# Up-weight sums kept in DRAM for the second token half, and the FFN's stores moved to the load queue

## The chip, the cores and the metric

The kernel runs on one core of one Trainium2 chip. The metric is the device time of one execution in microseconds (us); for the kernel before it is the median of three runs. TensorE (PE) does the matrix products, VectorE (DVE), ScalarE (ACT) and GpSimd (POOL) the elementwise work, and SyncE (SP) issues DMAs.

## The reference, cut to what matters

One layer of a diffusion backbone over 2048 tokens of width 1024. The first part (modulated RMSNorm, an input projection, neighbourhood attention, a gating block, a convolution block, an output projection, a residual) is not touched by the change. The second part is the FFN:

```
h2 = modulate(rmsnorm(x, norm2_g), mod_l[3], mod_l[4])        # 2048 x 1024
gate, up = split(h2 @ w_up, 2, axis=-1)                       # w_up: 1024 x 5632
gate = dwconv(gate, conv_w, conv_b)                           # 3 taps along the tokens
x = x + mod_l[5] * ((silu(gate) * up) @ w_down)               # w_down: 2816 x 1024
return rmsnorm(x, final_norm_g)
```

All arrays are float32. The kernel splits each float32 operand into a high part (a rounded copy) and a low part (what is left), and a product is made of three matmuls: high by high, high by low, low by high.

## The kernel before, in words

The FFN works on the tokens in two halves, `t` = 0 and 1, of 1024 tokens, which are two blocks of 512. The 44 column tiles of `w_up` (22 of the gate, 22 of up) are taken two by two: tile `c0` and tile `c0 + 11`. With the two blocks of tokens and the two halves of the 1024 input features this makes a 2 by 2 by 2 block product, and it is computed with seven products in place of eight (Winograd's form of Strassen's scheme). `winograd` issues the seven, each as twelve matmuls of 128 by 128 by 512 (`up_prod`, L1310), in the order B11, T2, T1, T3, B21, T4, B22. One such block of a gate tile and one of an up tile make a pair (`up_pair`), and there are eleven pairs in each half: 22 x 2 x 7 x 12 = 3,696 matmuls.

The scheme needs sums of the weights. `up_weights` loads the two tiles (`wa`, `wb`, 512 KB each, a double buffer), and POOL makes four sums `s1` to `s4` of 128 x 512 from their quarters (L1295 to L1298), through a ring `ws` of three buffers. Then each of the seven weight operands (three quarters as they are, four sums) is split by `halves`: ACT writes the high part (L1102), DVE the low part (L1103). The quarter `a21` goes into the sums alone. The weights and their sums are the same in both halves of the tokens; the kernel loads the weights and makes the sums twice.

The results of a gate block are put together on DVE in `gb` (L1321 to L1332), the convolution runs on ACT and DVE (L1363, L1365), and the product with up is made on DVE (L1370, L1375). `combine` makes the four sums of the activations that the down projection needs, on POOL (L1112 to L1115), and the seven tiles of a pair are stored to DRAM (`actd`, 256 KB each, L1381). Beside the pairs of the first half, `second_half` prepares the operands of the second half and stores them to DRAM (`td`); `reload` brings them back at the change of halves. Beside the pairs of the second half, `down_sums` loads the down weights (`wds`), makes their sums on DVE (L1270 to L1274) and stores them (`sd`). Its loads are ordered behind `last_w`, the load of the latest `wb` tile. After the 22 pairs the down projection reads `actd`, `sd` and `w_down`.

All loads go through `load`, which issues them from SP's queue. All stores go through `store`, on the engine that `phase(i)` has chosen from `CFG`; in the FFN this is POOL, whose DMA issues are instructions of POOL's own stream. `CFG` has two fields for a phase: the engines that take the low parts in `load_w`, and the engine of the stores.

The order of the instructions of each engine isn't the order of the program: a planner places them by a simulated timeline (L1639), and each engine then runs its own list in order. An instruction whose data aren't there holds up what stands behind it on its engine.

Of the kernel before, what the change touches and what calls it, by code (L numbers as in the profile page):

```python
# [10 lines left out]
F32 = mybir.dt.float32  # L11
F32R = mybir.dt.float32r
AF = mybir.ActivationFunctionType
ALU = mybir.AluOpType
# [4 lines left out]
P = 128  # L19
# [14 lines left out]
TB = 512  # L34
# [3 lines left out]
FT = 22  # L38
NP = FT // 2
# [104 lines left out]
def tile_hybrid_block(ctx: ExitStack, tc: tile.TileContext, a, out):  # L144
    nc = tc.nc

    cp = ctx.enter_context(tc.tile_pool(name="const", bufs=1))
    dp = ctx.enter_context(tc.tile_pool(name="scratch", bufs=1, space=DRAM))
# [36 lines left out]
    td = [dp.tile([P, 4, 2, TB], F32R, name=f"td{p}") if p in SPLIT else dp.tile([P, 4, TB], F32, name=f"td{p}")  # L185
          for p in range(7)]

    sd = [dp.tile([P, NP, 2, TB], F32, name=f"sd{j}") for j in range(2)]
    actd = [[dp.tile([P, NP, TB], F32, name=f"actd{t}{p}") for p in range(7)] for t in range(2)]

    def plain(ap):
        return ap.bitcast(F32) if ap.dtype == F32R else ap

    def load(dst, src):
        return nc.sync.dma_start(plain(dst), plain(src)).ins  # L195

    def store(dst, src):
        st_eng[0].dma_start(plain(dst), plain(src))
# [14 lines left out]

    flip = [0]
    E = {"P": nc.gpsimd, "V": nc.vector, "S": nc.sync, "A": nc.scalar}
    CFG = "V,P;PV,P;V,P".split(";")
    lo_engs = []
    st_eng = [None]

    def phase(i):  # L220
        l, st = CFG[i].split(",")
        lo_engs[:] = [E[x] for x in l]
        st_eng[0] = E[st]
# [876 lines left out]
    def halves(src, pool, tag, bufs, name, eng):  # L1100
        hl = pool.tile([P, 2, TB], F32R, tag=tag, bufs=bufs, name=name)
        nc.scalar.activation(hl[:, 0, :], src, AF.Copy)  # L1102
        eng.tensor_tensor(hl[:, 1, :], src, hl[:, 0, :].bitcast(F32), op=ALU.subtract)  # L1103
        return hl
# [174 lines left out]
    upn, last_w = [0], [None]  # L1279

    def up_weights(c0, name):

        if name in early:
            return early.pop(name)
        upn[0] += 1
        if upn[0] == 1:
            wa, wb = first_w
        else:
            wa, wb = ((w0p if upn[0] % 2 else fwb).tile([P, 1024], F32, tag=f"wst{upn[0] % 2}{i}", name=f"{name}{i}")
                      for i in range(2))  # L1290
            load(wa, a["w_up"][c0])
            last_w[0] = load(wb, a["w_up"][c0 + NP])
        a11, a12, a21, a22 = wa[:, 0:TB], wa[:, TB:], wb[:, 0:TB], wb[:, TB:]
        s1, s2, s3, s4 = (fw.tile([P, TB], F32, tag="ws", bufs=3, name=f"{name}s{i}") for i in range(4))
        nc.gpsimd.tensor_tensor(s1, a21, a22, op=ALU.add)  # L1295
        nc.gpsimd.tensor_tensor(s2, s1, a11, op=ALU.subtract)
        nc.gpsimd.tensor_tensor(s3, a11, a21, op=ALU.subtract)
        nc.gpsimd.tensor_tensor(s4, a12, s2, op=ALU.subtract)  # L1298
        return [halves(x, fw, "whl" if i > 1 else f"whl{i}", 4 if i > 1 else 1, f"{name}hl{i}", nc.vector)
                for i, x in enumerate((a11, s2, s1, s3, a12, a22, s4))]  # L1300

# [83 lines left out]
    def last_column():  # L1385
# [12 lines left out]
        nc.vector.tensor_tensor(b12, ue[:, NP:, 0], t2, op=ALU.subtract)  # L1398
        lastc.update({T2: t2, T1: t1, T3: t3, T4: b12, B22: b22})

    early["wg0_0"] = up_weights(0, "wg0_0")
    for p in (B21, T4, B22):
        open_comb(p)
    first_half_rest()
    sh, dw = second_half(), down_sums()
    for t in range(2):
        for k in range(NP):
            nm = f"{t}_{k}"
            up_pair(t, k, lambda: up_weights(k, "wg" + nm), lambda: up_weights(FT + k, "wu" + nm))
        if t == 0:  # L1410
            run_all(sh)
            reload()
# [9 lines left out]
    with ExitStack() as down:  # L1422
# [25 lines left out]
        for t in range(2):  # L1448
# [36 lines left out]
            def banks(tag, name):  # L1485
                return [dnp.tile([P, TB], F32, tag=tag, name=f"{name}{t}{i}") for i in range(4)]
# [53 lines left out]
            x = banks("x", "p1")  # L1540
# [4 lines left out]
            x = banks("x", "pu")  # L1545
# [88 lines left out]
def build(arrays_in, nc):  # L1634
    args = {}
    for name, v in arrays_in.items():
        args[name] = nc.dram_tensor("in_" + name, v.shape, F32, kind="ExternalInput").ap()
    out = nc.dram_tensor("out_0", (NB, P, KT, TB), F32, kind="ExternalOutput").ap()
    with tile.TileContext(nc, schedule_with_timeline_sim=True) as tc:  # L1639
        tile_hybrid_block(tc, args, out)  # L1640
# [12 lines left out]
```

## Time and profile before

| what | value |
|---|---|
| median of three runs | 2360.74 us (2357.55 to 2363.66) |
| profiled execution | 2365.48 us, span 2363.7 us |
| mean granted TensorE clock | 0.982 |
| busy, share of the span | PE 96%, DVE 72%, ACT 48%, POOL 34% |
| DMA | 473.63 MB, mean 200 GB/s |

Times in the trace are counted from the span's start. The first half's pairs run from about 1050 to 1475 us, the second half's from about 1475 to 1917 us, with some overlap at both ends, and the down projection fills the rest. An engine's busy share is an average over stages; what ends a stage is read from the waits in it. The granted clock is a share of 2.4 GHz.

### The profile page before, as it was taken

How to read it: one execution, taken by the hardware profiler on the slowest of the kernel's cores; microseconds unless marked ns; L12 is line 12 of the kernel's file. 1: busy time of each engine (PE TensorE's matmuls, PEld its weight loads, DVE VectorE, ACT ScalarE, POOL GpSimd, SP SyncE). 2: the span in 40 equal slices, each digit the busy share in tenths (PEclk: the TensorE clock that was granted, in tenths of full speed). 3: DMA queues.
4: the chain of work that ended last, by engine and by line, in shares of the span. 5: the costliest groups of instructions: out<-in, count | busy, mean ns of one | idle time of the engine just before them, and what ended most of it. 6: DMA issues, size and time to landing. Idle time of an engine off the chain costs nothing.

```text
span 2363.7 us, 34634 instructions
## 1 busy us (share of the span) xinstructions
PE 2268.4 (96%) x12474; PEld 1898.5 (80%) x12474; DVE 1710.7 (72%) x2552; ACT 1138.6 (48%) x2019; POOL 793.8 (34%) x844
## 2 busy tenths in 40 slices
PE   7999999999899899999999999999999999999998
PEld 5889777997788688878787788778788878888886
DVE  4787556556685694697888887788888777578565
ACT  4765643347455446564444443434333445454443
POOL 0255412111011132225566665455656432002000
PEclk8999999999999999999999999999999999999999
DMA  9675486557879679662444533745553368557653
GB/s 347 230 263 172 168 263 188 180 168 231 258 199 285 199 211 289 231 204 85 138 170 146 181 134 108 270 179 211 210 208 111 98 232 298 196 191 249 204 194 116
DMA packets 203868, 473.63 MB, mean 200 GB/s; under 512 B 21808, under 2 KB 70832, under 8 KB 202672
## 3 DMA queue, kind: packets, MB, share of 16 engines
q1 hardware_dynamic: 166160, 359.20, 47.5%
q0 software_dynamic: 31488, 105.93, 12.0%
q10 hardware_dynamic: 6048, 6.29, 0.8%
q8 instruction: 98, 1.61, 0.3%
q14 instruction: 74, 0.61, 0.1%
HBM read 352.06 MB, written 119.28 MB: 199 GB/s over the span
## 4 chain that ended last, share of the span: by engine, by line
PE 52%; DVE 15%; issue 13%; DMA 12%; ACT 4%; POOL 2%; SPq 1%; POOLq 0%; DVEq 0%; ACTq 0%
PE po L204 4%; PE p L1481 4%; PE pu L1481 4%; PE obank L204 3%; PE pk L204 3%; DMA adaf<-in_ada 3%; PE pv L1481 3%; PE s L204 2%; PE tp L210 2%; PE tp L204 2%; PE pq L204 2%; DMA wds<-in_w_down 2%; SPq L195 1%; DVE cv L575 1%; PE tg L204 1%
## 5 line engine op out<-in xcount | busy, mean ns | idle before, releaser
L575 DVE SCALAR_TENSOR_TENSOR cv<-hconv,cst,cv 128x512 f32<-128x512 f32 x240 | 215.6, 940 | 11.4 <-ACT cv L569 11.2
L1103 DVE TENSOR_TENSOR dw<-wd,dw 128x512 fp32r<-128x512 f32 x154 | 114.1, 749 | 103.3 <-ACT dw L1102 100.8
L1481 PE MATMUL pu<-ah,dw 128*128 128x512 f32 x792 | 181.7, 390 | 0.0
L698 ACT ACTIVATE sb<-sb,mx 128x544 f32<-128x544 f32 (+3 forms) x128 | 106.3, 830 | 154.8 <-DVE mx L695 148.8
L695 DVE CUSTOM_DVE_ANT_0 sb<-s,bias_t 128x544 f32<-128x544 f32 (+3 forms) x128 | 105.1, 821 | 101.7 <-PE s L204 78.3
L1481 PEld LDWEIGHTS pu<-ah,dw 128*128 128x128 f32 x792 | 148.7, 188 | 31.8 <-issue 1.0
L1102 ACT ACTIVATE dw<-wd 128x512 fp32r<-128x512 f32 x154 | 96.0, 628 | 159.7 <-PE pu L1481 58.3
L1481 PE MATMUL p<-ah,dw 128*128 128x512 f32 x528 | 122.5, 394 | 2.4 <-DVE u L1330 2.4
L1481 PE MATMUL pv<-ah,dw 128*128 128x512 f32 x528 | 120.3, 389 | 0.0
L1481 PEld LDWEIGHTS p<-ah,dw 128*128 128x128 f32 x528 | 100.2, 190 | 24.3 <-DVE u L1330 2.9
L204 PE MATMUL s<-kk,qq 128*128 128x256 f32 (+4 forms) x512 | 102.5, 323 | 16.3 <-DVE mx L695 10.2
L204 PEld LDWEIGHTS s<-kk,qq 128*128 128x128 f32 x512 | 89.5, 192 | 34.5 <-DVE mx L695 14.7
L1481 PEld LDWEIGHTS pv<-ah,dw 128*128 128x128 f32 x528 | 99.1, 188 | 20.6
L1367 ACT ACTIVATE c<-c 128x512 f32<-128x512 f32 x88 | 55.3, 630 | 124.9 <-DVE c L1365 124.6
L210 PE MATMUL tp<-cst,sb 128*128 128x128 f32 (+2 forms) x672 | 97.1, 275 | 13.0 <-DVE pt L730 9.0
L210 PEld LDWEIGHTS tp<-cst,sb 128*128 128x128 f32 (+2 forms) x672 | 79.9, 138 | 31.6 <-DVE pt L730 9.9
L1103 POOL TENSOR_TENSOR ah<-ra,ah 128x512 fp32r<-128x512 f32 x22 | 32.9, 1510 | 210.2 <-ACT ah L1102 208.8
L1102 ACT ACTIVATE ah<-ra 128x512 fp32r<-128x512 f32 x154 | 93.9, 617 | 10.6 <-DMA ra<-actd 10.5
L1103 DVE TENSOR_TENSOR ah<-ra,ah 128x512 fp32r<-128x512 f32 x132 | 92.2, 701 | 4.2 <-ACT ah L1102 4.2
L1365 DVE SCALAR_TENSOR_TENSOR cs<-gb,cst,cs 128x512 f32<-128x512 f32 x84 | 62.9, 749 | 21.9 <-ACT cs L1363 21.6
L728 ACT ACTIVATE pt<-tp 128x384 f32<-128x384 f32 (+2 forms) x128 | 61.2, 478 | 36.6 <-PE tp L210 36.0
L965 ACT ACTIVATE adaf<-adaf,silu_c 128x256 f32<-128x256 f32 x128 | 54.2, 497 | 50.5 <-DMA adaf<-in_ada 50.5
(1662 smaller groups left out, 7044.7 us busy)
## 6 DMA issues: line engine op xcount, KB each, us to landing
ra<-actd SPq DMA_DIRECT2D x70, 512.0 KB
wg<-in_w_up SPq DMA_DIRECT2D x44, 512.0 KB
wu<-in_w_up SPq DMA_DIRECT2D x44, 512.0 KB
actd<-tt POOLq DMA_DIRECT2D x88, 256.0 KB, 2.4
wd<-sd SPq DMA_DIRECT2D x40, 512.0 KB
actd<-c POOLq DMA_DIRECT2D x66, 256.0 KB, 2.4
adaf<-in_ada SPq DMA_DIRECT2D x32, 512.0 KB
qq<-qs SPq DMA_DIRECT2D x64, 256.0 KB
```

What stands on the lines that cost most here:

```text
L204: x = nc.tensor.matmul(*args, **kw)
L210: x = nc.tensor.transpose(*args)
L575: nc.vector.scalar_tensor_tensor(acc[ct], hb[:, ct, k:k + TB], cvw[:, ct, k:k + 1], acc[ct], op0=ALU.mult, op1=ALU.add)
L695: x = nc.vector.tensor_tensor_reduce(out=sb[:, w], in0=s[:, w], in1=bt[:, w], scale=-1.0, scalar=3.0e38, op0=ALU.add, op1=ALU.min, accum_o ...
L698: nc.scalar.activation(sb[:, w], sb[:, w], AF.Exp, bias=mx, scale=-1.0, accum_out=rs[:, cb, j:j + 1])
L728: nc.scalar.activation(dst, src, AF.Copy)
L965: nc.scalar.activation(t[:, k, :], t[:, k, :], AF.Copy, scale=silu_c[:, k0 + k, 0:1])
L1102: nc.scalar.activation(hl[:, 0, :], src, AF.Copy)
L1103: eng.tensor_tensor(hl[:, 1, :], src, hl[:, 0, :].bitcast(F32), op=ALU.subtract)
L1365: nc.vector.scalar_tensor_tensor(to, gb[:, i, o + d:o + d + TB], fcw[:, f, d:d + 1], ps, op0=ALU.mult, op1=ALU.add)
L1367: nc.scalar.activation(c, c, AF.Silu)
L1481: nc.tensor.matmul(ps[i], w[:, ww, sl], ah[:, aa, :], start=start and k_ == 0 and m == 0, stop=(k_ == NP - 1 and m == 2), skip_group_check ...
```

## The change: what it does

In the first half of the tokens `up_weights` works as before and also stores each of its four sums to a new DRAM array `su`, 256 KB each. In the second half it computes none of them: it loads the four from `su` into the same ring `ws`, in the order s2, s1, s3, s4. As `a21` is then not needed, only the right half of the `wb` tile (`a22`, 256 KB) is loaded. A fourth phase is added to `CFG`, in which the engine of the stores is SP, and it is chosen just before the FFN's first weights. So every `store` of the FFN (`td`, `actd`, `sd` and the new `su`) is issued by SP, in one list with the loads.

```diff
+    su = [dp.tile([FT, 4, P, TB], F32, name=f"su{j}") for j in range(2)]
...
-    CFG = "V,P;PV,P;V,P".split(";")
+    CFG = "V,P;PV,P;V,P;V,S".split(";")
...
         upn[0] += 1
+        t, x = divmod(upn[0] - 1, FT)
...
             load(wa, a["w_up"][c0])
-            last_w[0] = load(wb, a["w_up"][c0 + NP])
+            last_w[0] = load(wb, a["w_up"][c0 + NP]) if t == 0 else load(wb[:, TB:], a["w_up"][c0 + NP][:, TB:])
...
-        nc.gpsimd.tensor_tensor(s1, a21, a22, op=ALU.add)
-        nc.gpsimd.tensor_tensor(s2, s1, a11, op=ALU.subtract)
-        nc.gpsimd.tensor_tensor(s3, a11, a21, op=ALU.subtract)
-        nc.gpsimd.tensor_tensor(s4, a12, s2, op=ALU.subtract)
+        if t:
+
+            for i, x_ in ((1, s2), (0, s1), (2, s3), (3, s4)):
+                load(x_, su[x % 2][x, i])
+        else:
+            nc.gpsimd.tensor_tensor(s1, a21, a22, op=ALU.add)
+            nc.gpsimd.tensor_tensor(s2, s1, a11, op=ALU.subtract)
+            nc.gpsimd.tensor_tensor(s3, a11, a21, op=ALU.subtract)
+            nc.gpsimd.tensor_tensor(s4, a12, s2, op=ALU.subtract)
+            for i, x_ in enumerate((s1, s2, s3, s4)):
+                store(su[x % 2][x, i], x_)
...
+    phase(3)
     early["wg0_0"] = up_weights(0, "wg0_0")
```

## Rows read from the trace of the kernel before

**Rows 1.** The page's first part: busy time of each engine, share of the span, and its instructions.

```profile
PE 2268.4 (96%) x12474; PEld 1898.5 (80%) x12474; DVE 1710.7 (72%) x2552; ACT 1138.6 (48%) x2019; POOL 793.8 (34%) x844
```

**Rows 2.** Busy time by stretch: the first half's pairs, the second half's, the down projection. Columns: stretch and its length, then PE, PEld, DVE, ACT and POOL busy (x instructions), granted clock, DMA share, GB/s.

```profile
1000.00:1470.00 470.00, 459.70 (x1997) 377.40 (x1996) 401.69 (x509) 217.43 (x358) 268.65 (x309) 0.98 0.43 147
1470.00:1925.00 455.00, 441.36 (x1921) 361.52 (x1919) 373.15 (x487) 183.33 (x308) 243.50 (x268) 0.99 0.50 178
1925.00:2364.00 439.00, 425.70 (x1872) 351.05 (x1872) 292.53 (x421) 197.20 (x367) 45.66 (x35) 0.98 0.63 216
```

**Rows 3.** Waits of PE from 1000 to 1470 us, the three longest: us in total, times, longest.

```profile
PE g_5y L1310 <- DVE gb L1324: 2.8, 1, 2.8
PE g_2y L1310 <- DVE gb L1324: 2.2, 1, 2.2
PE g_6y L1310 <- DVE gb L1324: 1.9, 1, 1.9
```

**Rows 4.** Waits of PE from 1470 to 1925 us, all but the shortest.

```profile
PE g_0y L1310 <- DMA hh<-td: 3.0, 1, 3.0
PE g_1z L1310 <- DVE gb L1325: 3.0, 1, 3.0
PE g_4y L1310 <- DVE gb L1324: 2.6, 1, 2.6
PE g_5y L1310 <- DVE gb L1324: 2.0, 1, 2.0
PE u_3x L1310 <- ACT u_3p L1319: 1.3, 1, 1.3
PE u_10y L1310 <- DVE u L1324: 0.9, 1, 0.9
```

**Rows 5.** The chain that ended last, single pieces of PE: start us, us, what (x matmuls).

```profile
1151.25 4.57 PE g_2y L1310 x12
...
1270.87 4.61 PE g_5y L1310 x12
...
1312.55 4.61 PE g_6y L1310 x12
...
1485.55 3.90 PE g_0y L1310 x11
1489.45 3.22 PE u_10y L1310 x12
...
1509.21 2.72 PE g_0y L1310 x12
```

**Rows 6.** DVE's and POOL's instructions in order of time around 1553 us: start us, us, engine, line, operation, out<-in.

```profile
1552.53 5.47 DVE L1103 TENSOR_TENSOR wu_1hl<-wu,wu_1hl 128x512 fp32r<-128x512 f32 x1
...
1551.86 1.31 POOL L1113 TENSOR_TENSOR tt<-c,tt 128x512 f32<-128x512 f32 x1
1553.12 1.30 POOL L1114 TENSOR_TENSOR tt<-c,c 128x512 f32<-128x512 f32 x1
...
1554.94 1.29 POOL L1296 TENSOR_TENSOR wg_2s<-wg_2s,wg 128x512 f32<-128x512 f32 x1
1556.17 1.27 POOL L1115 TENSOR_TENSOR tt<-c,tt 128x512 f32<-128x512 f32 x1
```

**Rows 7.** The same around 1668 and 1709 us; the brackets give the idle time of the engine just before and what ended it.

```profile
1668.17 3.08 DVE L1270 TENSOR_TENSOR wds<-wds,wds 128x512 f32<-128x512 f32 x1 [4.53 <-DMA wds<-in_w_down]
...
1668.51 1.30 POOL L1115 TENSOR_TENSOR tt<-c,tt 128x512 f32<-128x512 f32 x1
...
1708.78 3.33 DVE L1270 TENSOR_TENSOR wds<-wds,wds 128x512 f32<-128x512 f32 x1 [3.84 <-DMA wds<-in_w_down]
...
1708.46 1.30 POOL L1115 TENSOR_TENSOR tt<-c,tt 128x512 f32<-128x512 f32 x1
```

**Rows 8.** Busy time of the instructions of L1103 alone (the low parts): stretch, its length, DVE busy (x), POOL busy (x), clock, DMA share, GB/s. First half, second half, down projection.

```profile
1070.00:1470.00 400.00, 159.05 (x157) 0.00 (x0) 0.99 0.41 140
1530.00:1910.00 380.00, 136.53 (x133) 0.00 (x0) 1.00 0.47 169
2000.00:2300.00 300.00, 134.84 (x208) 17.13 (x11) 1.00 0.62 207
```

**Rows 9.** POOL's time at two lines, in the same form: its DMA issues (L198) in the first half, then one of the four sums (L1298) in the second.

```profile
1070.00:1470.00 400.00, 54.06 (x98) 0.99 0.41 140
...
1480.00:1925.00 445.00, 29.27 (x22) 0.99 0.50 179
```

**Rows 10.** Busy time by stretch at the change of halves; columns as in rows 2.

```profile
1480.00:1490.00 10.00, 6.97 (x25) 5.33 (x24) 8.63 (x12) 4.23 (x7) 5.97 (x8) 0.84 1.02 382
1490.00:1500.00 10.00, 10.00 (x45) 8.19 (x45) 5.59 (x10) 3.65 (x6) 4.32 (x8) 0.99 1.04 394
```

**Rows 11.** DMA prices: a store from POOL (KB each, median us from issue to landing), and the time that SP takes to issue a weight load (ns min/median/max, first and last start).

```profile
actd<-tt POOLq DMA_DIRECT2D x88, 256.0 KB, 2.4
...
L195 SPq DMA_DIRECT2D wu<-in_w_up x44: 327/332/933, 1051.4 to 1871.0; - x44
```

**Rows 12.** SP's issues in order of time around one pair of the second half, and DVE's total wait for the `wds` loads from 1480 to 1925 us (us, times, longest).

```profile
1657.62 2.71 SPq L195 DMA_DIRECT2D wg<-in_w_up  x2
1660.43 2.03 SPq L195 DMA_DIRECT2D wds<-in_w_down  x2
...
DVE wds L1270 <- DMA wds<-in_w_down: 15.8, 7, 4.5
```

## Prediction, written before the result was known

> **What bounds the kernel now.** I read the busy line first: PE has 96% of the span, DVE 72%, POOL 34% [rows 1]. The change touches only the FFN's up part, so the next view is busy time by stretch. In both halves PE is at 97 to 98%, DVE at 82 to 85%, POOL at 54 to 57%; in the down projection PE is also at 97% with POOL nearly idle [rows 2]. So nothing here is bound by POOL or by the DMA share (0.43 and 0.50). What the change can win is the time in which PE stands, and what follows from it. The waits of PE list that time: three waits on DVE in the first half, 2.8 + 2.2 + 1.9 = 6.9 us [rows 3]; in the second, 3.0 us on a reload and 3.0 + 2.6 + 2.0 + 1.3 + 0.9 = 9.8 us on DVE and ACT [rows 4]. A wait of PE can cost more than itself: twelve matmuls take 2.72 us in the undisturbed row, but 4.57, 4.61 and 4.61 us behind the three waits of the first half, and 3.90 (for eleven) and 3.22 behind the reload [rows 5]. That is the lower of TensorE's two clocks, 1.2 in place of 2.4 GHz, granted for a few us (the stretch of 1480 to 1490 shows a mean clock of 0.84 [rows 10]); it adds 1.85 to 1.89 us per wait. All of it together is 6.9 + 5.6 in the first half, 3.0 + 1.9 at the reload, and 9.8 + 1.9 behind it: 29 us, 1.2% of the time. That is the ceiling of the gain.
>
> The view in order of time says why DVE is late. One low part that takes some 0.68 us elsewhere took 5.47 us: it began while POOL ran a tensor operation, and four of them followed each other on POOL until 1557.4; DVE ended at 1558.0 [rows 6]. Over the halves a low part takes 159.05/157 = 1.01 us and 136.53/133 = 1.03 us, but 134.84/208 = 0.65 us in the down projection, where POOL is nearly idle [rows 8]. So POOL's tensor operations stretch DVE's operations by about a third of a microsecond each.
>
> The Trainium skill (SBUF — State Buffer, "Who interferes with whom") gives the mechanism as an exclusive lock: a DVE operation with two SBUF inputs and a GpSimd operation share one pair of ports, and the later one blocks until the other has ended. By one lock per operation the 5.47 us would have been at most 0.68 plus what was left of one POOL operation, about 2 us; the row is longer, so POOL kept the pair through several. With one lock per operation the first term below would be 3 x 1.3 + 1.9 = 5.8 in place of 8.8 us and the result 2356 us; I go by the measured rows.
>
> **The change part by part.**
>
> *Sums off POOL in the second half.* 22 weight blocks times four sums go. One costs 29.27/22 = 1.33 us [rows 9], so 88 x 1.33 = 117 us of POOL's 243.5 us [rows 2] leave. POOL is not the bound; the gain is that DVE is blocked less. POOL keeps as many tensor operations in `combine` (44 in eleven pairs), so about half of the stretching stays. Per wait: in the 5.47 us case the sum of L1296 (1.29 us) and the DMA issues between the four operations leave, which brings POOL's end from 1557.4 to about 1555.0, so 2.5 of the 3.0 us of wait go. The waits of 2.6 and 2.0 us have another beginning: DVE stood 4.53 and 3.84 us for a `wds` load, and then its operation took 3.08 and 3.33 us beside POOL's L1115 [rows 7]. The load's part stays. The stretch (3.08 - 0.68 = 2.4, 3.33 - 0.68 = 2.65) goes if POOL's L1115 has ended by then; without the sums and the issues in front of it it would have begun about 2 us earlier, so I take both stretches as gone, 2.4 + 2.0. The others (1.3, 0.9) I leave. With one low-clock stretch of 1.9: 2.5 + 2.4 + 2.0 + 1.9 = 8.8 us gained. Ends: 0 (other stalls appear in their place) and 11.7 (all).
>
> *Stores off POOL's stream.* In the first half 98 issues, 54.06 us [rows 9], leave POOL; SP has room, since its issues take 0.33 us [rows 11]. But POOL's tensor operations there stay all 88, so the locks stay, and may come closer together without issues between them. Of the 12.5 us of the first half I take 2 as gained. Ends: all 12.5 gained, and two new waits of the price of the longest, 2 x (2.8 + 1.9) = 9.4 us lost.
>
> *New stores in the first half.* 22 x 4 x 256 KB = 23 MB beside a DMA share of 0.43 [rows 2]; with a store landing in 2.4 us [rows 11] a sum is in DRAM long before its buffer is written again, which waits for ACT and DVE to have split it. I take nothing; its upper end is in the SP term.
>
> *New loads in the second half.* Per weight block four loads of 262 KB come and half of `wb`, 262 KB, goes: +0.79 MB, 17 MB in all, over 440 us, on a share of 0.50. In the pairs this is hidden: a sum is needed some 10 us after its buffer is free. It isn't at the change of halves, where DMA runs at 382 to 394 GB/s with a share of 1.02 to 1.04 [rows 10] and PE already waits 3.0 us for a reload [rows 4]. Two blocks fall into that stretch: 2 x 0.79 / 0.385 = 4.1 us of transfer. PE has matmuls of the last pair of the first half to fill in, so I take half, 2 us lost. Ends: 0 and 4.1 + 1.9 (a longer low clock) = 6.
>
> *Waits added to SP's list.* A store on SP waits for its data, and the loads behind it wait with it. Behind it stand weight loads, `x1d` and `wds` loads and the reload; weights are double-buffered and come a whole block ahead, so a few us there cost nothing. The `wds` loads are tight: they follow the weight loads by a few us [rows 12], land at 4.5 and 3.8 us too late in the worst cases [rows 7], DVE waits 15.8 us for them in seven of eleven cases [rows 12], and behind DVE's wait stands the sum that PE needs. For them the smaller `wb` load (0.26 MB less in front, about 0.7 us at 385 GB/s) speaks for the change, a store of `actd` that waits for `combine` against it. The trace of before shows no store on SP. Ends: 2 us gained, and 20 us lost (worked out under the second rival). I take 1 us lost, nearest to the weight loads, which are most of what stands there.
>
> Sum: -8.8 - 2 + 2 + 1 = -7.8 us. The profiled execution took 2365.48 us, 4.7 us (0.2%) above the median, so the sum gives 2357.7 for it, and 2353 us on the median of 2360.74.
>
> **The rivals.** *No change.* DVE is relieved, but PE's waits are single events of which each needs a chance meeting, and a new order of the planner makes others; the terms of the second half and the first cancel with those of the reload and SP: about 2360, between 2354 and 2367. For it: DVE's busy share of 82 to 85% already leaves PE at 97 to 98% [rows 2], so another 35 us off DVE buys little. Against it: the three largest waits of the second half all show a stretched operation [rows 6, 7].
>
> *Slower: stores hold up the loads in one list.* The place is the `wds` load and the reload. `combine` runs for four POOL operations, about 5.2 us, before its last store can go. If a `wds` load stands behind such a store, it comes later by up to that. Take 2.7 us, half of it, on the ten `wds` steps that have a pair's store near, and pass 2 us of each on to PE, as in the 2.6 of 4.53 us case [rows 4, 7]: 20 us lost, less 8.8 gained: +11, 2372 us. It decides from the point where DVE's wait for `wds` grows from 15.8 to over 30 us. For it: SP's order is fixed by the planner, whose timeline already misses the `wds` landing by 4.5 us. Against it: with less on POOL, `combine` ends earlier.
>
> The Trainium skill (DMA: Bandwidth & Descriptors, "Queues, rings and completion order") says that DMA engines take turns between queues, and within one queue work in order. By it the seven `actd` stores of the last pair, 1.8 MB or 4.8 us at 385 GB/s, stand in front of the reload instead of beside it. That is a loss of up to 4.8 us inside this rival's 11, and no row here shows it, as all stores were on another queue.
>
> *The sums come too late from DRAM.* Then POOL's 1.3 us per sum is exchanged for a wait of ACT at L1102 on each block: 22 x 1 us = 22 us, less 8.8: 2374 us. Three buffers for four sums speak for it, the early free time against it.
>
> **How the numbers follow.** This kernel's measurement can tell about 0.3% (7 us) from no change. The forecast, gains that outweigh the costs, has 0.44 (2353; its own range 2338 to 2354), no change 0.30, the one-list rival 0.18, the late sums 0.08. The range 2338 to 2376 leaves out about 2 in 10: a gain near the ceiling of 29 us and slow cases beyond the second rival.
>
> **What would show it.** POOL's busy time in the second half falls to about 243 - 117 - 55 = 70 us; L1103's mean there falls from 1.03 to about 0.8 us; the PE waits at g_1z, g_4y and g_5y shrink or go; PE's wait at the reload grows to about 5 us. Wrong: DVE's `wds` wait over 30 us, waits of ACT at L1102 for `su`, PE waits in the first half above 7 us, or a second half that is not shorter though L1103's mean has fallen.

## The result, and the profile after

The changed kernel took 2332.22 us (median of four runs, 2331.53 to 2335.09); the kernel before, run beside it, 2361.61 us (four runs, 2357.55 to 2363.66). The ratio is 0.988, with a 95% interval of 0.9863 to 0.9897: 29.4 us gained. The forecast was 2353 us, its range 2338 to 2376; the time lies below the range, and the gain is nearly four times the forecast 7.8 us. It is as large as the 29 us that the prediction had called the ceiling; that the two agree so well is partly luck, as the lengths below show.

Code after the change stands a few lines lower: L1320 is the old L1310, L1334 the old L1324, L1105 the old L1103, L1272 the old L1270, L200 the store and L197 the load.

The page's busy line of the changed kernel, which answers to [rows 1]:

```profile
PE 2255.0 (97%) x12474; PEld 1889.2 (81%) x12474; DVE 1621.2 (70%) x2552; ACT 1139.8 (49%) x2019; POOL 584.1 (25%) x552
```

PE and DVE run as many instructions as before and DVE is still busy 90 us less; POOL loses 210 us and 292 instructions. The two stretches of the up part, with the columns of [rows 2]:

```profile
1000.00:1470.00 470.00, 464.94 (x2044) 382.91 (x2044) 385.26 (x527) 225.92 (x371) 225.35 (x211) 0.99 0.60 207
1470.00:1925.00 455.00, 449.56 (x1977) 370.28 (x1977) 319.65 (x487) 184.70 (x308) 84.69 (x84) 1.00 0.66 228
```

In 470 us PE now gets 47 matmuls more done than in the same stretch before, in 455 us 56 more. The DMA share rose from 0.43 to 0.60 and from 0.50 to 0.66, and no wait of PE on a transfer came of it. The longest waits of PE, first half and then second, which answer to [rows 3] and [rows 4] (us, times, longest):

```profile
PE g_0x L1320 <- DVE hl L1135: 1.6, 2, 1.3
PE g_2y L1320 <- DVE gb L1334: 1.6, 1, 1.6
```

```profile
PE u_3z L1320 <- DVE wu_3hl L1105: 1.6, 1, 1.6
PE p L1492 <- DVE u L1340: 1.6, 1, 1.6
PE u_10y L1320 <- DVE u L1334: 0.9, 1, 0.9
```

The waits of 1.9 to 3.0 us are gone in both halves, the one for the reload among them. The change of halves, which lay in the stretches of [rows 10] before, now lies about 16 us earlier; PE is full there and its clock granted in full:

```profile
1460.00:1470.00 10.00, 10.00 (x46) 8.28 (x45) 8.29 (x13) 4.20 (x7) 0.96 (x3) 1.00 0.99 355
1470.00:1480.00 10.00, 10.00 (x45) 8.28 (x45) 5.50 (x10) 4.06 (x7) 3.68 (x6) 1.00 1.05 394
```

The low parts alone, columns of [rows 8], first half, second half, down projection:

```profile
1060.00:1460.00 400.00, 138.98 (x163) 0.00 (x0) 1.00 0.58 199
1500.00:1880.00 380.00, 102.97 (x138) 0.00 (x0) 1.00 0.62 211
1970.00:2270.00 300.00, 135.64 (x209) 17.13 (x11) 1.00 0.62 207
```

That is 0.85, 0.75 and 0.65 us for one, where the kernel before had 1.01, 1.03 and 0.65. The fall in the first half is the surprise: POOL's 88 sums and 44 operations of `combine` are all still there.

To compare kernels I use three figures from each trace: the length of each half of the up part (the first from the end of the first up matmul to the end of the last matmul of `u_10` of the first half, the second from there to the end of the last one of the second half), and the number of DVE operations in each that last 2 us or more. One profiled execution stands behind each length. The down projection, where the code is the same in nearly all, took 438.2 to 440.9 us in these kernels. The part ahead of the FFN varies more: the first up matmul starts between 996.3 us (e6) and 1007.2 us (e9), with the same code in front.

| kernel | FFN stores from | sums of the second half | time, us | first half | second half | DVE operations of 2 us and more |
|---|---|---|---|---|---|---|
| before | POOL | POOL | 2361.6 | 491.9 | 428.0 | 13, 14 |
| changed | SP | DRAM | 2332.2 | 476.4 | 417.8 | 0, 0 |
| e1_stores_sp | SP | POOL | 2352.5 | 474.4 | 439.7 | 0, 0 |
| e2_sums_only | POOL | DRAM | 2348.0 | 482.4 | 421.7 | 14, 0 |
| e3_su_sp | `su` SP, others POOL | DRAM | 2350.5 | 482.0 | 424.1 | 12, 0 |
| e4_stores_act | ACT | DRAM | 2347.0 | 481.5 | 420.4 | 0, 0 |
| e5_pool_issues | SP, 204 extra from POOL | DRAM | 2355.0 | 483.5 | 425.2 | 8, 0 |
| e6_before_resident | POOL | POOL | 2353.6 | 488.3 | 424.3 | 13, 10 |
| e7_stores_sp_resident | SP | POOL | 2336.0 | 474.6 | 418.8 | 0, 0 |
| e8_after_resident | SP | DRAM | 2337.0 | 476.6 | 414.6 | 0, 0 |
| e9_after_pool_mult | SP | DRAM, and 88 operations on POOL | 2354.0 | 475.7 | 432.9 | 0, 0 |
| e10_out_sp | SP, one phase more | DRAM | 2333.6 | 473.6 | 419.1 | 0, 0 |
| e11_all_sp | SP, two phases more | DRAM | 2335.7 | 473.4 | 420.2 | 0, 0 |

In the profiled executions the first half became 15.5 us shorter and the second 10.2, 25.7 together. As measured here, the first half holds the wait for the reload too, which in the kernel before ends at 1485.55 us [rows 5], ahead of the last matmul of `u_10`. Another 7.0 us lie where the code is the same: 4.9 us ahead of the FFN and 2.1 in the down projection. About half of these come from the choice of executions, as the profiled one of the kernel before is 3.9 us above its median and that of the changed kernel 0.6; they are not a gain of the change.

### The profile page after: what moved, and what is told of

It reads as the page before. It is cut to its first block, busy times and chain, and to the rows that moved or that the text cites. A ratio compares the mean times of both kernels' runs of the same rounds, so it can differ in the third digit from the quotient of the medians.

```text
span 2331.0 us, 34996 instructions
## 1 busy us (share of the span) xinstructions
PE 2255.0 (97%) x12474; PEld 1889.2 (81%) x12474; DVE 1621.2 (70%) x2552; ACT 1139.8 (49%) x2019; POOL 584.1 (25%) x552
## 5 line engine op out<-in xcount | busy, mean ns | idle before, releaser
L1105 DVE TENSOR_TENSOR dw<-wd,dw 128x512 fp32r<-128x512 f32 x154 | 111.7, 732 | 102.0 <-ACT dw L1104 101.7
L1105 DVE TENSOR_TENSOR ah<-ra,ah 128x512 fp32r<-128x512 f32 x132 | 92.0, 700 | 1.7 <-ACT ah L1104 1.7
L1105 POOL TENSOR_TENSOR ah<-ra,ah 128x512 fp32r<-128x512 f32 x22 | 32.6, 1499 | 210.2 <-ACT ah L1104 208.9
L732 DVE COPY pt<-tp 128x256 f32<-128x256 f32 (+1 forms) x128 | 57.5, 450 | 24.6 <-PE tp L212 24.2
```

Source lines behind the costliest of these rows:

```text
L732: nc.vector.tensor_copy(dst, src)
```

## Experiments

### The two parts by themselves

`e1_stores_sp` moves the stores and leaves the sums on POOL in both halves, with the whole `wb` tile loaded in both; `e2_sums_only` keeps the sums in DRAM and leaves the stores on POOL.

```diff
# e1, against the changed kernel
-        if t:
+        if False:
...
-            for i, x_ in enumerate((s1, s2, s3, s4)):
-                store(su[x % 2][x, i], x_)
# e2, against the changed kernel
-    CFG = "V,P;PV,P;V,P;V,S".split(";")
+    CFG = "V,P;PV,P;V,P;V,P".split(";")
```

> Half of the change: the FFN's stores on SP, the sums made on POOL in both halves and nothing kept in DRAM. Theory I (what held DVE up were POOL's DMA issues among its tensor operations; they leave): most of the 29 us gain stays, 2338 to 2345 us, mean of L1103 in the first half near 0.85 us as after the change, PE waits on DVE in the first half under 4 us. Theory S (the sums on POOL were the cost): little stays, 2352 to 2362 us. Theory O (the planner's new order of instructions, not a price of any operation): the time may land anywhere between, and the means of L1103 don't follow it.

> The other half: the sums kept in DRAM and loaded in the second half, all FFN stores (88 more, of the sums) issued by POOL. Theory I: the first half gets worse, since 88 more issues of 0.55 us stand on POOL there, and the second half better by some 9 us as predicted: 2350 to 2362 us. Theory S: most of the gain is here: 2335 to 2345 us.

Measured, with the kernel before at 2363.01 us beside them: e1 2352.50 us, ratio 0.9953 (0.9931 to 0.9975); e2 2348.04 us, ratio 0.9929 (0.9906 to 0.9953). So 10.5 and 15.0 us, 25.5 together, near the 29.4 of the whole change. e1 came out where theory S had it, by its time, but its first half is as theory I said: 17.5 us shorter, with low parts of 141.91/163 = 0.87 us. e2 came out between the two, and its first half did not get worse with 88 more issues. By halves the parts don't add at all. e1 loses 11.7 us in the second half, where these waits of PE, and of DVE for the `wds` loads, stand (L1317, L1331 and L1271 are L1320, L1334 and L1272 of the changed kernel):

```profile
PE g_4y L1317 <- DVE gb L1331: 3.0, 1, 3.0
PE g_3y L1317 <- DVE gb L1331: 2.7, 1, 2.7
```

```profile
DVE wds L1271 <- DMA wds<-in_w_down: 28.3, 9, 5.3
DVE wds L1271 <- issue: 5.8, 2, 3.6
```

DVE waits 34.1 us for `wds`, in place of 15.8 [rows 12]. This is the prediction's second rival at work: the stores in the list of the loads make the `wds` loads late. SP stands in that list at the stores of `sd`, until DVE has made their sums (SP, 1480 to 1925 us; the kernel before has no store on SP):

```profile
SPq L199 <- DVE wds L1274: 44.1, 11, 5.6
SPq L199 <- DVE wds L1275: 21.6, 11, 3.3
```

e2 has the wait for the reload again, and waits of 3.1 and 2.4 us in the first half:

```profile
PE u_4x L1320 <- ACT u_4p L1329: 3.1, 1, 3.1
PE g_7y L1320 <- DVE gb L1334: 2.4, 1, 2.4
```

```profile
PE g_0y L1320 <- DMA hh<-td: 2.4, 2, 1.4
```

### The late loads of the down weights

DVE in the changed kernel waits for `wds` nearly as long as in e1, and PE hardly notices (its wait of 1.6 us at u_3z stands right behind the longest of DVE's, 4.8 us):

```profile
DVE wds L1272 <- DMA wds<-in_w_down: 26.9, 10, 4.8
```

Here the stores on SP are not what makes them late. e2, whose stores POOL issues, has nearly the same wait, and so has e4, whose stores ACT issues (25.3 us); what the three have in common, against the kernel before, are the loads of the sums. The line of e2:

```profile
DVE wds L1272 <- DMA wds<-in_w_down: 24.8, 11, 5.3
```

To see what that wait is worth, three kernels do away with it: the four DVE sums of `down_sums` are replaced by eight operations of 240 columns on a tile that is always there. The sums of the down weights are left out in these three.

```diff
-            nc.vector.tensor_tensor(a22, a21, a22, op=ALU.add)
-            nc.vector.tensor_tensor(a21, a11, a21, op=ALU.subtract)
+            for op in (ALU.subtract, ALU.add, ALU.subtract, ALU.add):
+                nc.vector.tensor_tensor(dm, dm, u[:, 0, 0:240], op=op)
...
-            nc.vector.tensor_tensor(a11, a22, a11, op=ALU.subtract)
-            nc.vector.tensor_tensor(a12, a12, a11, op=ALU.subtract)
+            for op in (ALU.subtract, ALU.add, ALU.subtract, ALU.add):
+                nc.vector.tensor_tensor(dm, dm, u[:, 0, 0:240], op=op)
```

> The kernel before, with the four DVE operations per step of down_sums replaced by eight of 240 columns on a tile that is always there; the wds tiles are loaded and stored as they are, so the sums of the down weights are left out. DVE's work stays about the same, its wait for the wds loads goes. Theory W (in the second half PE stands because DVE waits for a late wds load and then works on stretched): the two PE waits at g_4y and g_5y go, 5 to 8 us less than before. Rival (the stretching by POOL alone): the time stays within 3 us of before.

> The same replacement in the kernel of e1_stores_sp (stores on SP, sums made on POOL in both halves), whose second half was 11.7 us longer than before; the sums of the down weights are left out here too. Theory W: that loss is DVE's wait for wds loads that come later behind the stores, so 15 to 20 us go: 2332 to 2340 us. Rival (the loss comes from POOL's tensor operations standing closer together): 2347 to 2355 us.

> The same replacement in the changed kernel; the sums of the down weights are left out. Theory W: DVE's 26.9 us of waits for wds cost PE almost nothing there, since an unstretched DVE catches up, so at most 4 us go: 2328 to 2333 us. If wds waits cost something by themselves, 10 us go.

Measured, the kernel before at 2361.43 us: e6 (in the kernel before) 2353.57, ratio 0.9965 (0.9953 to 0.9978); e7 (in e1) 2336.01, ratio 0.9888 (0.9867 to 0.9909); e8 (in the changed kernel) 2337.03, ratio 0.9899 (0.9878 to 0.9919). The same edit is worth 16.5 us in e1, 7.9 in the kernel before and nothing in the changed kernel. e6 and e7 came within what theory W expected, although in e6 the wait at g_4y only shrank, from 2.6 to 2.2 us; e8 lies above its 2328 to 2333 us, without a gain. In e7 the second half fell from 439.7 to 418.8 us and no wait of PE on a `gb` is over 0.2 us, although POOL still makes the sums and a low part still takes 129.54/140 = 0.93 us there:

```profile
1500.00:1880.00 380.00, 129.54 (x140) 0.00 (x0) 1.00 0.50 172
```

So neither the late loads alone (changed kernel) nor the stretched operations alone (e7) stop PE for long. It takes both. One thing stays open: the edit also lets the stores of `sd` go without DVE, so that SP's 65.7 us at them (e1) are gone in e7 as well. How much of the gain in e7 belongs to DVE's own wait, and how much to the loads that no longer stand behind these stores, is not separated. The counterpart puts the POOL operations back into the changed kernel, on the sums that have been loaded:

```diff
             for i, x_ in ((1, s2), (0, s1), (2, s3), (3, s4)):
                 load(x_, su[x % 2][x, i])
+                nc.gpsimd.tensor_tensor(x_, x_, unit.to_broadcast([P, TB]), op=ALU.mult)
```

> The changed kernel, with a product by one on POOL for each of the 88 sums that the second half loads (128x512, in place): POOL's tensor operations of the second half are back, all else is the change. If POOL's tensor operations in the second half are what costs (they stretch DVE, and DVE then passes its wds waits on to PE): L1103's mean there returns to about 0.88 us and 8 to 18 us are lost, 2340 to 2350 us. Rival (the kernel e1 lost its time by the full wb loads and the planner's order): 2331 to 2336 us.

Measured: 2353.97 us, ratio 0.9963 (0.9949 to 0.9976), more than the 2340 to 2350 expected, while a low part there rose only to 115.49/141 = 0.82 us, not to 0.88. With the 88 operations the second half grew by 15.1 us, to 432.9, and these waits came (PE, then DVE):

```profile
PE g_4y L1321 <- DVE gb L1335: 3.0, 1, 3.0
PE g_3y L1321 <- DVE gb L1335: 2.8, 1, 2.8
```

```profile
DVE wds L1272 <- DMA wds<-in_w_down: 21.1, 6, 4.2
DVE wds L1272 <- issue: 13.7, 3, 6.7
```

They are the waits of e1 over again, at g_3 and g_4, on `gb` and not on one of the sums that the added operation delays. That fits this reading of what the sums in DRAM are for: not POOL's time, but DVE's room to make up for a late load.

### Who issues the stores

`e4_stores_act` lets ACT issue them. `e5_pool_issues` leaves the stores on SP and adds an issue of 64 KB on POOL beside each of 204 of them (not for `su`). `e3_su_sp` gives SP the 88 stores of `su` and leaves the others on POOL.

```diff
# e4
+    CFG = "V,P;PV,P;V,P;V,A".split(";")
# e5, in store
+        if again and st_eng[0] is nc.sync:
+            nc.gpsimd.dma_start(extra.pop(), part)
# e3
+    CFG = "V,P;PV,P;V,P;V,P".split(";")
+                nc.sync.dma_start(su[x % 2][x, i], x_)
```

> The whole change, but the FFN's stores issued by ACT in place of SP (292 issues, some 0.33 us each on an engine with a busy share under 50%). Theory I: what counts is that POOL doesn't issue, so the time stays at 2330 to 2340 us. Rival (it is the one list of loads and stores on SP that brings the order of the transfers, above all the earlier reload at the change of halves): 2345 us or more, with PE waiting for td again.

> The whole change, and beside each of the 204 stores of td, actd and sd on SP a second store of its first 128 columns, issued by POOL into scratch (64 KB each): POOL's issues and their waits are back, the sums of the second half are not. Theory I: about the part of the gain that the stores brought is lost, 2342 to 2352 us, and L1103's mean in the first half returns to about 1.0 us. Theory S: 2330 to 2337 us.

> The changed kernel, but of the FFN's stores only the 88 of the sums (su) are issued by SP; the 98 others of the first half and those of the second are issued by POOL again. Theory 'POOL's issues cost in the first half': POOL issues as many stores there as in the kernel before, so the first half keeps two or three waits of PE on DVE of 1.5 us and more, the mean of the low parts there is near that of the kernel before (0.97 to 1.0 us), and the time is near that of the kernel with the sums alone, 2342 to 2350 us. Rival 'only their number with the sums' stores counts': the 88 stores are what e2 has more than the changed kernel, so the first half falls to that of the changed kernel (mean of the low parts 0.84 us, no wait above 1.6 us) and the time is 2332 to 2337 us. In both, PE's wait for the reload at the change of halves is there again, 2 to 3 us, if the stores on POOL are what brings it.

Measured: e4 2346.98 us, ratio 0.993 (0.9907 to 0.9954); e5 2354.98, ratio 0.9961 (0.9946 to 0.9976); e3 2350.45, ratio 0.9953 (0.9934 to 0.9972), the kernel before at 2361.47 beside it. The longest waits of PE behind DVE in the first half, of e5 and then of e3 (the wait of g_0x at its beginning left out):

```profile
PE g_5y L1325 <- DVE gb L1339: 4.6, 1, 4.6
PE g_2y L1325 <- DVE gb L1339: 2.5, 1, 2.5
```

```profile
PE u_5z L1320 <- DVE wu_5hl L1105: 3.1, 1, 3.1
PE g_2y L1320 <- DVE gb L1334: 2.2, 1, 2.2
PE g_5y L1320 <- DVE gb L1334: 1.7, 1, 1.7
```

Issues on POOL whose data nobody reads bring the long waits at g_2 and g_5 back (e5), and so do the old ones without the 88 of `su` (e3), so the rival in e3's expectation, that only the sums' stores count, falls. Its last sentence fell too: e3 has no wait for the reload. In time both came somewhat above what was expected. In e5 the mean of the low parts did not return to 1.0 us, it is 139.34/159 = 0.88, and yet eight DVE operations last 2 us and more; what PE meets are these single operations and not the mean.

e4 fell into the range of its rival (2345 us or more), but without the rival's sign: PE does not wait for `td` there. ACT as the issuer has no long DVE operation, like SP, but waits of its own. Its store issues wait for their data, and its operations on `gb` stand behind them (the profile puts this down to the stores):

```profile
ACT gb L1361 <- DMA actd<-tt: 8.8, 3, 3.8
```

Its first half is 481.5 us. So it isn't enough for the first half that POOL doesn't issue; the engine that does must not hold up what PE needs. All waits of PE from 1000 to 1470 us add up to 4.5 to 5.4 us in the seven kernels whose stores SP issues without POOL (the changed kernel, e1, e7 to e11), and to 10.0 to 13.3 us in the other six. That speaks against theory O of e1, by which the order of the instructions and no price of an operation would decide.

`e10_out_sp` and `e11_all_sp` go on in the same direction, to beat the changed kernel: the stores of one and of two earlier phases on SP as well (`"V,P;PV,P;V,S;V,S"`, `"V,P;PV,S;V,S;V,S"`).

> The changed kernel with the 30 stores of x1d of the output projection's phase issued by SP as well, in place of POOL (30 x 0.55 us = 16.5 us off POOL's stream). Theory 'an issue on POOL costs only where DVE is held up by POOL's tensor operations and PE waits for DVE': POOL is busy for a quarter of that stretch or less and DVE has little to be held up by, so nothing changes, 2328 to 2336 us. Rival 'every issue on POOL delays something': 98 issues of the first half were worth some 12 us, so 30 are worth 3 to 4 us, 2328 us, with the gain before 1050 us. Rival 'one list': the x1d stores stand in front of the first weight loads of the FFN and the change costs 3 to 10 us, 2335 to 2342.

> As the run before, and the stores of the phase ahead of it (attention and what follows) issued by SP too; there the low parts are shared between POOL and DVE. Theory 'an issue on POOL costs only where DVE is held up and PE waits for DVE': POOL makes low parts there that PE waits for, and about 100 issues of 0.55 us leave its stream, so a gain of 0 to 10 us, all before 900 us: 2322 to 2332. Rival 'one list': in that stretch the DMA share is 0.7 to 0.8, higher than in the FFN, stores that wait for results hold up loads that PE needs, and the time grows by 5 to 30 us, 2337 to 2362.

Measured: 2333.61 us, ratio 0.988 (0.9863 to 0.9898), and 2335.65 us, ratio 0.9881 (0.9862 to 0.9901): no change. e10 came as its first theory had it. For e11 neither a gain nor a loss can be told. None of those that compute the whole is faster than the changed kernel.

### What an issue on POOL does to DVE

In the kernel before, all 27 DVE operations of 2 us and more in the up part (the first at 1147.71 us with 2.89 us, the last at 1820.07 us with 4.09 us) lie beside an issue of POOL, which runs during the operation or has ended less than 1.5 us before it; together they are 57.3 us longer than 0.68 us each. None occurs in a half whose FFN stores POOL has no part in, whatever the number of POOL's operations. None occurs either in the second halves of e2, e3 and e5, where POOL issues some 98 stores but runs only 44 tensor operations: it seems to take both, close together. The same operation in both kernels, in order of time, DVE and POOL (start us, us). Before:

```profile
1260.15 0.55 POOL L198 DMA_DIRECT2D td<-tbs  x1
1260.67 3.14 DVE L1103 TENSOR_TENSOR wg_5hl<-wg_5s,wg_5hl 128x512 fp32r<-128x512 f32 x1
1260.71 1.30 POOL L1113 TENSOR_TENSOR tt<-c,tt 128x512 f32<-128x512 f32 x1
1261.96 1.28 POOL L1114 TENSOR_TENSOR tt<-c,c 128x512 f32<-128x512 f32 x1
```

After:

```profile
1251.71 1.63 POOL L1115 TENSOR_TENSOR tt<-c,tt 128x512 f32<-128x512 f32 x1
1252.11 1.79 DVE L1105 TENSOR_TENSOR wg_5hl<-wg_5s,wg_5hl 128x512 fp32r<-128x512 f32 x1
1253.31 1.74 POOL L1116 TENSOR_TENSOR tt<-c,c 128x512 f32<-128x512 f32 x1
```

After, POOL's operations last 1.6 to 1.75 us and DVE gets one operation done in each: they take turns. Before, two of POOL's run through at 1.3 us and DVE ends 0.56 us behind the second. Two small kernels measure this by themselves. They compute nothing of the reference: DVE subtracts without a pause, and beside it POOL adds, with other instructions between the additions.

> Not the FFN but a small kernel by itself, which computes nothing of the reference: 48 subtractions of 128 x 512 on DVE without a pause in each of seven stretches (dv0 to dv6), beside them on POOL: nothing (0), 16 additions of 128 x 512 (1), 16 additions each followed by a DMA issue of its result (2), 16 additions each followed by a memset of 128 x 256 (3), 16 DMA issues alone (4), eight times two additions and two issues (5), eight times issue, addition, addition (6). In the traces of the FFN a DVE operation lasts 2 us or more (through two POOL operations) 27 times in the kernel before, and always with a DMA issue of POOL in it, and never in the halves without POOL issues, where POOL and DVE take turns (1.7 us each). Theory 'the issue lets POOL go first twice': operations of 2 us and more come in stretches 2, 5 and 6, none in 0, 1, 3 and 4; in stretch 1 they are 0.68 or some 1.8 us. Rival 'any pause of POOL does it': stretch 3 has them too. Rival 'the issue itself holds DVE': stretch 4 has operations of 1.2 us and more. Rival 'it needs what stands around it in the FFN' (the matmuls, the ACT writes or the waits there): no stretch has any of 2 us and more.

> The small kernel again, with POOL's instructions kept in the order written, as the planner had moved the memsets and some of the issues of the run before away from the additions. Beside 48 subtractions of DVE per stretch POOL now runs 16 additions: alone (adds), each followed by a memset of 128 x 400 of some 0.5 us (memsets), each by its DMA issue (issues), every second by an issue (pairs), every fourth by four issues (quads), each by a copy of one column (copies), and nothing (alone). Theory 'an issue makes POOL go first': DVE's operations last 1.63 us in adds, 2 us at most in memsets and copies, and some 3.5 us in pairs and longer in issues, or at least 2 us; in quads one operation lasts through all four additions, some 6 us. Rival 'any pause of POOL does it, since DVE then begins before POOL': memsets and copies have operations of 2 us and more as well.

In e12 the planner moved the memsets to the front and gathered the issues by twos, so only some of its stretches are what was meant: additions alone gave DVE operations of 1.63 us at most, two additions and two issues in turn 3.65 us, and issues alone (184.0 to 192.7 us) left all 13 at 0.69. e13 kept the order. Its DVE operations by stretch (ns min/median/max, first and last start; each stretch has 48, of which only the first part has POOL beside it, so the longest, the last of the three durations, is the one to read):

```profile
L59 DVE TENSOR_TENSOR adds<-a,e x48: 691/693/1633, 4.9 to 53.7; 128x512 f32<-128x512 f32 x48
L59 DVE TENSOR_TENSOR memsets<-a,e x48: 692/693/1632, 56.6 to 106.7; 128x512 f32<-128x512 f32 x48
L59 DVE TENSOR_TENSOR issues<-a,e x48: 691/693/2266, 109.6 to 167.1; 128x512 f32<-128x512 f32 x48
L59 DVE TENSOR_TENSOR pairs<-a,e x48: 692/693/3342, 169.9 to 225.4; 128x512 f32<-128x512 f32 x48
L59 DVE TENSOR_TENSOR quads<-a,e x48: 692/693/1719, 228.2 to 281.4; 128x512 f32<-128x512 f32 x48
L59 DVE TENSOR_TENSOR copies<-a,e x48: 692/693/1774, 284.2 to 336.4; 128x512 f32<-128x512 f32 x48
```

And one period of "pairs":

```profile
175.64 6.71 DVE L59 TENSOR_TENSOR pairs<-a,e 128x512 f32<-128x512 f32 x2
178.72 0.56 POOL L35 DMA_DIRECT2D dst<-po  x1 [0.30 <-POOL po L39]
179.30 2.49 POOL L39 TENSOR_TENSOR po<-a,b 128x512 f32<-128x512 f32 x2
```

One issue ahead of two additions lets both go through in 2.49 us, and DVE gets one operation of 3.3 us done for two of POOL's, where additions alone give it one for each. A memset of 0.43 us or a copy of one column in the issue's place doesn't do this. They leave a shorter pause between two additions, 0.34 and 0.54 us, than the issue, 0.87 us. But e1 has pauses of 0.68 us in POOL without an issue, and there the operation that begins first also ends first, and POOL is the one that waits:

```profile
1223.26 0.68 DVE L1104 TENSOR_TENSOR tbs<-tb,tbs 128x512 fp32r<-128x512 f32 x1
1223.47 1.62 POOL L1303 TENSOR_TENSOR wg_5s<-wg_5s,wg 128x512 f32<-128x512 f32 x1 [0.68 <-POOL wg_5s L1302]
```

In "pairs" DVE begins 0.28 us ahead of POOL's addition too, while the issue runs, and lasts 3.3 us. So nothing is left that speaks for the rival that any pause does it; a pause of just 0.87 us without an issue was not tried.

The expectation was wrong for "quads": after four issues in a row DVE's operations last 1.72 us at most, not some 6. These stretches show one more thing. Beside each group of issues that additions follow, DVE has an operation of 1.63 us though POOL's record has issues alone (those that begin at 237.2, 245.6 and 254.1 us); beside the last group, which no addition follows, DVE stays at 0.69 us. It looks as if an addition that stands behind an issue can hold DVE up before its own record begins. How POOL comes by the second turn is not shown, and the profile calls its own spans on POOL rough; what is shown, by DVE's durations, is that a single issue close ahead of its operations gives it one.

## Why the prediction was wrong, step by step

**What bounds the kernel, and the ceiling.** Right. What could be won was the time in which PE stood and the low clock behind it, 29 us; the up part won 25.7 us in the profiled executions, and of the waits that made up the ceiling only single ones of 1.6 us are left. The granted clock of the two stretches rose from 0.98 and 0.99 to 0.99 and 1.00.

**Stores off POOL's stream, taken as 2 us gained: the step that failed.** It said that "POOL's tensor operations there stay all 88, so the locks stay, and may come closer together without issues between them". The operations stayed and what they do to DVE didn't: the low parts of the first half fell from 1.01 to 0.85 us, and no DVE operation lasts 2 us any more. With issues on POOL the first half takes 482.0 to 491.9 us (before, e2, e3, e5, e6; mean 485.6), with the stores on SP alone 473.4 to 476.6 us (the changed kernel, e1, e7 to e11; mean 475.0). The lengths of the kernel before and of e6 hold the reload's wait and the low clock behind it, 3.0 + 1.9 and 2.8 + 1.9 us (the 1.9 taken over for e6), which are another term. Without them the term is 8.7 us by the means, and 15.5 - 4.9 = 10.6 in the pair of kernels that was to be forecast, in place of 2; the prediction's own upper end was 12.5. The row was there to be read: in [rows 6] the operation of 5.47 us lay through four POOL operations, with an issue in the middle of them, where the rows have a line of dots:

```profile
1554.35 0.57 POOL L198 DMA_DIRECT2D actd<-tt  x1
```

The prediction took the issues as time lost to POOL, not as what lets it go first.

The Trainium skill (SBUF — State Buffer, "Who interferes with whom") gives an exclusive lock for the length of one instruction. e13's additions agree with it, one operation waiting for one other (1.63 us). With an issue in between (3.34 us) the measurement differs from it, and decides. Its section "SBUF: two separate sides" tells of DVE, during an operation in a 2-port mode, keeping POOL from writing descriptors. In this case the issues took their 0.55 us as ever and it was DVE that waited.

How the length of DVE's operations comes to PE is seen at g_5. From its first sum on `gb` to the second (L1321 to L1324, now L1331 to L1334) DVE runs the same operations. The rows of that tile, before and after (duration ns min/median/max, first and last start us):

```profile
L1321 DVE TENSOR_TENSOR gb<-g_5p,g_5y x1: 677/677/677, 1257.2 to 1257.2; 128x512 f32<-128x512 f32 x1
L1324 DVE TENSOR_TENSOR gb<-g_5p,g_5y x1: 676/676/676, 1270.1 to 1270.1; 128x512 f32<-128x512 f32 x1
```

```profile
L1331 DVE TENSOR_TENSOR gb<-g_5p,g_5y x1: 683/683/683, 1248.0 to 1248.0; 128x512 f32<-128x512 f32 x1
L1334 DVE TENSOR_TENSOR gb<-g_5p,g_5y x1: 672/672/672, 1258.9 to 1258.9; 128x512 f32<-128x512 f32 x1
```

12.9 us before, 10.9 after. PE's wait of 2.8 us there [rows 3] is gone.

**Sums off POOL in the second half, taken as 8.8 us gained.** The second half became 10.2 us shorter, and the waits at g_1z, g_4y and g_5y went, as forecast; POOL is busy 84.7 us (about 70 said) and a low part takes 0.75 us (0.8 said). The step holds, but it isn't a term by itself: with the stores on POOL the sums in DRAM are worth 3.9 us (428.0 to 424.1 in e3) to 8.7 us (to 421.7 in e2, of which 2.4 are the reload's wait, which falls into the second half there), with the stores on SP 21.9 us (439.7 to 417.8).

**The reload, taken as 2 us lost.** Wrong in its sign, and the second largest part of the miss: the wait of 3.0 us and the low clock behind it (1.9) are gone, 6.9 us away from the forecast. The transfers are as dense as I assumed (394 GB/s), but the first load of `hh` is now issued 2.0 us ahead of the first matmul of the second half (1456.48 and 1458.49 us) and was issued 1.6 us behind it (1475.69 and 1474.10). I had costed the bytes and left the planner's new order out. The wait is there in the kernel before, e2 and e6 and in no other; e3, with most stores on POOL, is without it, so the engine of the stores doesn't settle it. What does settle it was not tried.

**New stores, and new loads within the pairs, nothing.** Right in what they cost PE. ACT does wait for sums from DRAM, one of the prediction's signs of being wrong: 49.7 us in thirteen waits, the longest 7.9 us. No wait of PE in the second half is put down to one of them, so the fourth case (late sums) is out:

```profile
ACT wg_4hl L1104 <- DMA wg_4s<-su: 7.9, 1, 7.9
```

**Waits in SP's list, taken as 1 us lost, and the one-list rival.** For the changed kernel about right: the late `wds` loads cost PE one wait of 1.6 us, and taking them away gains nothing in time (e8). The rival's mechanism is real all the same. Without the sums in DRAM (e1) DVE waits 34.1 us for `wds`, beyond the 30 us that the prediction named, and the second half loses 11.7 us; in e7, without that wait, it is 20.9 us shorter again. So the second part of the change pays for a loss that the first part brings, and the prediction, which added the two as if they were independent, could not see it. The rival "no change" needed new stalls in the place of the old; none came.

**The sum.** In the pair of profiled executions the terms measure 10.2 (sums), 10.6 (stores) and 4.9 us (reload) gained, 25.7, against 8.8 and 2 gained and 3 lost. The rest of the way to the 29.4 us between the medians is the difference where the code is the same, so it is luck that the gain matches the ceiling. A gain near the ceiling was among the cases that the range left out knowingly.

## What to carry to other kernels

Where DVE is the engine that feeds PE and POOL works beside it, count POOL's DMA issues as well as its operations: an issue just ahead of two POOL operations can make DVE wait for both, and stores that SP issues don't. Stores moved into the list of the loads, and new loads as well, make other loads late (DVE's wait for `wds` grew from 15.8 to 34.1 and to 24.8 us); whether that costs anything depends on how much room the waiting engine has, so judge such an edit together with whatever else loads that engine. And when a wait of PE goes, count the low clock behind it: the ceiling of the gain is the sum of the waits and of these stretches, and here most of it was reached.

## What was not expected of the hardware

A DVE operation with two inputs in SBUF takes 0.69 us alone, 1.63 us beside POOL additions without a pause, and 3.3 us beside pairs of additions with one DMA issue ahead of each pair, though POOL does no more work there. POOL's additions last 1.24 us each (2.49 for two) behind an issue and 1.64 where they take turns (26.26 us for 16 in e13). Issues alone leave DVE at 0.69 us where no addition follows them; with additions to follow, one operation beside them took 1.63 us ("quads").
